# A hybrid decoder layer on one core: block substitution to 32, its scratch copies on the weights' queue, a diagonal by column sums, and steps in another order

## The chip, the cores and the metric

The kernel runs on one core of one Trainium2 chip. The metric is the device time of one launch in microseconds (us). The kernel before took 1806.01 us (median of three runs, 1805.75 to 1806.58).

## The reference, cut to what matters

One decoder layer for 256 positions of width 2048, all in fp32. Three branches (a gated DeltaNet A, an HGRN2 recurrence B, attention C into 256 memory rows) share one input projection; their outputs are projected back, gated, merged and projected again, and an MLP of width 8192 follows.

```
proj = h @ w_in[l]                        # 2048 x 15376
...
lower = where(strict, bc[..., :, None] * einsum('bhnid,bhnjd->bhnij', kc, kc) * dec, 0.0)
a_mat = lower + eye(CHUNK)
sol = lax.linalg.triangular_solve(a_mat, rhs, left_side=True, lower=True, unit_diagonal=True)   # branch A
...
a_i = einsum('bhtd,bhjd,bhtjd->bhtj', q_i, k_i, dec)                                            # branch B
o = (q_i * exp(b_i)) @ state + a_i @ v_i
...
merged = ga * (oa @ w_br_a[l]) + gb * (ob @ w_br_b[l]) + gc * (oc @ w_br_c[l])
x = x + rmsnorm(merged @ w_out[l], g_post_mix[l])
m = square(relu(h2 @ w_mlp_in[l])) @ w_mlp_out[l]
x = x + rmsnorm(m, g_post_mlp[l])
```

The change touches two pieces: the inverse of the unit triangular `a_mat` in branch A (the kernel works with chunks of 128, so one 128x128 matrix for each of 8 heads and 2 chunks), and, in branch B, the diagonal of `a_i`, where the decay is 1, so that it is the sum over d of q times k.

## The kernel before, in words

**The products with the weights.** Nearly all of the time TensorE multiplies activations with weights. Each fp32 number is split into a high and a low part (fp32r), and three products (high x high, high x low, low x high) are summed. Weights come in groups of 512 KB (two K-tiles of 128 rows by 512 columns). For each group SyncE issues one DMA into one of four raw buffers `w` (L163), ScalarE writes the high part `wh` (L174), VectorE subtracts to get the low part `wl` (L175), and both parts have four buffers of their own. A `unit` (L206 to L208) spends 12 matmuls of 128x512 on a group; a `unit_joined` (L225, L227) spends 8 of 128x512 and 8 of 128x256. All weights go through SyncE's one queue, in program order.

**The branches' own work.** Everything else of the branches (convolutions, norms, chunk matrices, recurrences) is written as Python generators. After each weight group `tick` adds a rate (R1 to R4, by stage) to a credit and runs that many steps of the generator at hand, so that small work is dealt out between the groups. A scheduler then orders each engine's instructions for itself, except those that are wrapped in `pin`. What an engine has in its list, it does in that order: a VectorE step that waits holds back the `wl` behind it.

**Branch A** (`gen_a`) runs in two halves (hg 0 and 1), each of 4 heads x 2 chunks = 8 matrices. It writes the signed strict triangles `U`, then inverts: (1) the eight 16x16 diagonal blocks `U[k,:,k]` go to a DRAM scratch `scr` (8 DMAs, L849) and come back as `Lb`, each block copied to 16 partitions (8 DMAs of 128 KB, L851), both on GpSimd's queue; (2) VectorE substitutes: 15 pairs of a product (L885) and a sum (L886), each for all heads and blocks at once; (3) TensorE transposes the result (L896), and three turns s = 16, 32, 64 double the block: `pw` (L916, for s = 64 L905), `pzt` (L921, L910), then for s < 64 eight transposes into `X` (L929), with a copy on VectorE or ScalarE behind each.

**Branch B** (`gen_b`) works in two halves too. Its diagonal comes from eight fp32 matmuls of 128x128, k against q (`ad`, L1064), of which a mask keeps the diagonal.

**The opening** makes five small turns on TensorE (`rb` by two, the gate column, `pc`, `pl`), each with a bank of its own, between the first weight groups; `dec` (L798) is a pair of matmuls with the triangle `mgtr` for each chunk.

Of the kernel before, what the change touches and what calls it, by code (L numbers as in the profile page):

```python
# [10 lines left out]
F32 = mybir.dt.float32  # L11
# [22 lines left out]
KG = 2  # L34
BL = 16
WB = 4
R1, R2, R3, R4 = 1.1, 1.0, 1.0, 1.2


@with_exitstack  # L40
def tile_trunk(ctx: ExitStack, tc, a):
# [361 lines left out]


    mgt, mlt, caus = const("mgt", [P, P]), const("mlt", [P, P]), const("caus", [P, P])
    mgtr = const("mgtr", [P, P], F32R)
    msk2 = const("msk2", [P, 2, P])
    dblk = const("dblk", [P, BL])
    mblk = const("mblk", [P, P])
    mT = {s: const(f"mT{s}", [P, P]) for s in (1, 2, 4, 8, 16, 32, 64)}  # L410

    def gen_masks():
        G.affine_select(out=mgt, in_=ones, pattern=[[-1, P]], base=0, channel_multiplier=1,
                        compare_op=ALU.is_gt, fill=0.0)
        G.affine_select(out=mlt, in_=ones, pattern=[[1, P]], base=0, channel_multiplier=-1,
                        compare_op=ALU.is_gt, fill=0.0)
        pin(V.tensor_tensor(out=caus, in0=mlt, in1=ident, op=ALU.add))
        pin(V.tensor_copy(mgtr, mgt))
        pin(V.tensor_copy(msk2[:, 0, :], mlt))
        pin(V.tensor_scalar(out=msk2[:, 1, :], in0=caus, scalar1=-1.0, scalar2=None, op0=ALU.mult))  # L420
        pin(V.tensor_reduce(out=dblk, in_=ident.rearrange("p (k c) -> p c k", c=BL), axis=AX.X, op=ALU.add))
        yield
        prev = ident
        for s in (1, 2, 4, 8, 16, 32, 64):
            b = 2 * s
            if b < P:
                cur = mblk if b == BL else cst.tile([P, P], F32, tag=f"blk{b.bit_length() % 2}", name=f"blk{b}")
# [10 lines left out]
            pin(V.tensor_tensor(out=mT[s], in0=d, in1=mlt, op=ALU.mult))  # L438
            prev = cur
            yield  # L440

# [27 lines left out]
    def gen_start():  # L469
# [14 lines left out]
        adma(lrow, a["lb_raw"][0].rearrange("(c p) -> c p", p=P))  # L484
        load_x()
        yield
        pb = bank("rb")
        for t in range(NT):
            rr = g4("rr", (P, P))
            V.tensor_scalar(out=rr, in0=ones, scalar1=rsm[:, t:t + 1], scalar2=None, op0=ALU.mult)  # L490
            T.matmul(pb[:, t * P:(t + 1) * P], rr, ident, start=True, stop=True)
        V.tensor_copy(rbm, pb[:, 0:S])
        yield
        load_x()
        turn_grow(grow, 32, 16)
        yield
        pc = bank("pc")
        T.transpose(pc[:, 0:96], crow, ident[0:96, 0:96])
        V.tensor_copy(ccol, pc[:, 0:96])
# [6 lines left out]
        pl = bank("pl")  # L506
        T.transpose(pl[:, 0:8], lrow, ident[0:8, 0:8])
# [262 lines left out]
    def gen_a(hg, kc, qc, vc, z):  # L770
# [20 lines left out]
        dec = g4("dec", (P, 8, P))  # L791
        for t in range(NT):
            dl = g4("dl", (P, 2, 4, P), F32R)
            pd = bank("dec")
            for i, l_ in enumerate((ldh, ldl)):
                V.tensor_tensor(out=dl[:, i], in0=bc(caus, 4),
                                in1=l_.bitcast(F32)[:, t, hs].unsqueeze(2).to_broadcast([P, 4, P]), op=ALU.mult)
                T.matmul(pd, mgtr, dl[:, i].rearrange("p h i -> p (h i)"), start=i == 0, stop=i == 1)  # L798
            A.activation(dec[:, t * 4:t * 4 + 4, :], pd.rearrange("p (h i) -> p h i", h=4), AF.Exp)
            yield  # L800
# [20 lines left out]
        for t in range(NT):  # L821
# [13 lines left out]
            for h in range(4):  # L835
# [5 lines left out]
                if h % 2 == 1:  # L841
                    yield

        NB = P // BL
        scr = dp.tile([NB, 8, BL, BL], F32, tag="scr", name=nm("scr"))
        Lb = lp.tile([P, 8, BL * BL], F32, tag="lb", name=nm("lb"))
        for k in range(NB):
            sl = slice(k * BL, (k + 1) * BL)
            pin(G.dma_start(scr[k].rearrange("b c m -> c b m"), U[sl, :, sl]))  # L849
        for k in range(NB):  # L850
            G.dma_start(Lb[k * BL:(k + 1) * BL].rearrange("p b m -> p (b m)"),  # L851
                        scr[k:k + 1].rearrange("k b c m -> k (b c m)").to_broadcast([BL, 8 * BL * BL]))
        yield
        ct0, cp0 = small("ct0", 4), small("cp0", 4)
        V.tensor_tensor(out=ct0, in0=cneg[:, 0:4], in1=t0e[:, hs], op=ALU.mult)
# [19 lines left out]

        X, XT, W = g4("X", (P, 8, P)), g4("XT", (P, 8, P)), g4("W", (P, 8, P))
        V.memset(W, 0.0)
        V.memset(Lb[:, :, 0:BL * BL:BL + 1], 1.0)
        Xc = lp.tile([P, 8, BL], F32, tag="xc", name=nm("xc"))
        V.tensor_copy(Xc, dblk.unsqueeze(1).to_broadcast([P, 8, BL]))  # L880
        yield
        for c in range(BL - 2, -1, -1):
            n = BL - c
            tm = lp.tile([P, 8, BL], F32, tag="tm", name=nm("tm"), bufs=2)
            V.tensor_tensor(out=tm[:, :, 0:n], in0=Xc[:, :, c:BL], in1=Lb[:, :, c * BL + c:(c + 1) * BL], op=ALU.mult)  # L885
            V.tensor_reduce(out=Xc[:, :, c], in_=tm[:, :, 0:n], axis=AX.X, op=ALU.add)  # L886
            if c % 2 == 0:
                yield
# [151 lines left out]
    def gen_b(hg, k, g, q, v, z):  # L1040
# [382 lines left out]
```

## Time and profile before

| What | Value |
|---|---|
| median of three runs | 1806.01 us (1805.75 to 1806.58) |
| the profiled execution | 1806.44 us |
| its span in the trace | 1804.7 us |
| TensorE busy | 1793.5 us, 99% of the span |
| VectorE busy | 1127.0 us, 62% |
| ScalarE busy | 905.6 us, 50% |
| mean granted clock of TensorE | 0.999 |

The profiled execution is 0.43 us above the median, and 1.7 us longer than its span. In the trace's rows, a start and a duration in us stand first, then the engine, the line, the operation and its tiles; "wl<-w,wh" reads: writes `wl`, reads `w` and `wh`. A matmul's printed duration holds its latency, and matmuls overlap; what one costs in a row of many is the distance from its start to the next one's. TensorE's fp32 matmuls are recorded twice (x16 for eight). A window's row has, for each engine, its busy us and the number of its instructions, then the granted clock, the DMA engines' busy share and the bytes moved per second.

### The profile page before, as it was taken

Reading aid. Unit: us, or ns where it says so; the run is one execution under the profiler, and the core shown is the slowest. Engines: PE = TensorE matmul, PEld = TensorE weight load, DVE = VectorE, ACT = ScalarE, POOL = GpSimd, SP = SyncE. Lnnn points to the kernel's source line nnn. Section 1 sums busy time; section 2 is a strip of 40 time slices with the busy share of each in tenths; the row PEclk is TensorE's granted clock in tenths of the full one; section 3 lists DMA queues with packets and bytes.
Section 4 is the critical chain, followed back from the end, with each engine's and each line's share of the span. In section 5 each row is a group of like instructions: output and inputs, shape, how many; then the busy total and the mean of one; then the engine's idle time right before and its main releaser. Section 6 shows DMA issues by size and latency. Waiting matters only on the chain.

```text
span 1804.7 us, 23851 instructions
## 1 busy us (share of the span) xinstructions
PE 1793.5 (99%) x9241; PEld 1532.6 (85%) x9241; DVE 1127.0 (62%) x1518; ACT 905.6 (50%) x1156; POOL 44.5 (2%) x68
## 2 busy tenths in 40 slices
PE   9999999999999999999999999999999999999998
PEld 7888888888888888888888888888888888888886
DVE  5865678755764677696555557655655565655556
ACT  6645565544555565555444445544444444444433
POOL 1000000200200000000000000000000000000000
PEclk9999999999999999999999999999999999999999
DMA  8665645754665556465666674666666676666664
GB/s 264 207 194 160 185 146 168 209 172 138 177 187 152 158 169 187 141 186 175 198 186 187 213 232 152 191 193 191 195 186 198 188 220 187 195 187 195 188 194 139
DMA packets 174946, 333.40 MB, mean 185 GB/s; under 512 B 13144, under 2 KB 14832, under 8 KB 174576
## 3 DMA queue, kind: packets, MB, share of 16 engines
q1 hardware_dynamic: 169280, 325.10, 58.7%
q10 hardware_dynamic: 4528, 4.54, 0.9%
q0 software_dynamic: 1024, 2.23, 0.7%
q8 instruction: 72, 1.18, 0.3%
q14 instruction: 42, 0.34, 0.1%
HBM read 329.60 MB, written 2.23 MB: 184 GB/s over the span
## 4 chain that ended last, share of the span: by engine, by line
PE 97%; DVE 1%; DMA 1%; ACT 1%; issue 0%; SPq 0%; DVEq 0%; POOLq 0%; POOL 0%; ACTq 0%
PE mm L225 23%; PE mm L206 18%; PE mm L207 18%; PE mm L208 18%; PE mm L227 12%; PE pa L1120 1%; DMA w<-in_w_kv_mem 0%; PE pzt L921 0%; PE pw L916 0%; PE mm L373 0%; PE mm L375 0%; PE mm L372 0%; DVE wl L175 0%; DMA w<-in_w_in 0%; DVE cv L718 0%
## 5 line engine op out<-in xcount | busy, mean ns | idle before, releaser
L175 DVE TENSOR_TENSOR wl<-w,wh 128x1024 fp32r<-128x1024 f32 x600 | 728.5, 1223 | 540.2 <-ACT wh L174 456.3
L174 ACT CAST wh<-w 128x1024 fp32r<-128x1024 f32 x600 | 628.0, 1052 | 719.0 <-PE mm L208 453.7
L206 PE MATMUL mm<-wh,hh 128*128 128x512 f32 x576 | 227.5, 395 | 0.3 <-DVE sum L266 0.3
L208 PE MATMUL mm<-wh,hh 128*128 128x512 f32 x576 | 224.7, 390 | 0.0
L225 PE MATMUL mm<-h2h,wh 128*128 128x512 f32 x960 | 224.4, 390 | 0.0
L207 PE MATMUL mm<-wl,hh 128*128 128x512 f32 x576 | 224.4, 390 | 0.0
L225 PEld LDWEIGHTS mm<-h2h,wh 128*128 128x128 f32 x960 | 178.3, 188 | 35.8
L206 PE MATMUL mm<-wh,mh 128*128 128x512 f32 x512 | 199.2, 389 | 0.0
L207 PE MATMUL mm<-wl,mh 128*128 128x512 f32 x512 | 199.2, 389 | 0.0
L208 PE MATMUL mm<-wh,ml 128*128 128x512 f32 x512 | 199.2, 389 | 0.0
L225 PE MATMUL mm<-hh,wh 128*128 128x512 f32 x768 | 184.8, 391 | 0.3 <-ACT z L730 0.3
L225 PEld LDWEIGHTS mm<-hh,wh 128*128 128x128 f32 x768 | 141.0, 188 | 27.8 <-ACT z L730 0.5
L208 PEld LDWEIGHTS mm<-wh,hh 128*128 128x128 f32 x576 | 108.1, 188 | 22.7
L206 PEld LDWEIGHTS mm<-wh,hh 128*128 128x128 f32 x576 | 108.2, 188 | 21.8 <-DVE sum L266 0.5
L207 PEld LDWEIGHTS mm<-wl,hh 128*128 128x128 f32 x576 | 108.3, 188 | 21.1
L227 PEld LDWEIGHTS mm<-h2h,wl 128*128 128x128 f32 x960 | 119.3, 192 | 2.3
L227 PE MATMUL mm<-h2h,wl 128*128 128x256 f32 x960 | 120.3, 283 | 0.0
L207 PEld LDWEIGHTS mm<-wl,mh 128*128 128x128 f32 x512 | 96.1, 188 | 20.0
L208 PEld LDWEIGHTS mm<-wh,ml 128*128 128x128 f32 x512 | 96.1, 188 | 19.9
L206 PEld LDWEIGHTS mm<-wh,mh 128*128 128x128 f32 x512 | 96.1, 188 | 19.9
L227 PE MATMUL mm<-hh,wl 128*128 128x256 f32 x768 | 102.2, 284 | 0.0
L227 PEld LDWEIGHTS mm<-hh,wl 128*128 128x128 f32 x768 | 98.9, 191 | 3.4
(388 smaller groups left out, 1913.9 us busy)
## 6 DMA issues: line engine op xcount, KB each, us to landing
w<-in_w_in SPq DMA_DIRECT2D x240, 512.0 KB, 4.0
w<-in_w_mlp_in SPq DMA_DIRECT2D x128, 512.0 KB, 4.0
w<-in_w_mlp_out SPq DMA_DIRECT2D x128, 512.0 KB, 4.2
w<-in_w_out SPq DMA_DIRECT2D x32, 512.0 KB, 4.1
w<-in_w_kv_mem SPq DMA_DIRECT2D x30, 512.0 KB, 4.9
w<-in_w_br_c SPq DMA_DIRECT2D x16, 512.0 KB, 4.1
w<-in_w_br_a SPq DMA_DIRECT2D x16, 512.0 KB, 4.5
w<-in_w_br_b SPq DMA_DIRECT2D x16, 512.0 KB, 3.6
```

What stands on the lines that cost most here:

```text
L174: q(A.copy(wh[:, js, 0:width], w[:, js, 0:width]))
L175: q(V.tensor_tensor(out=wl[:, js, 0:width], in0=w[:, js, 0:width], in1=wh.bitcast(F32)[:, js, 0:width], op=ALU.subtract))
L206: T.matmul(o, st, wh[:, j, :], start=kt == 0, stop=False)
L207: T.matmul(o, st, wl[:, j, :], start=False, stop=False)
L208: T.matmul(o, sl, wh[:, j, :], start=False, stop=kt == nk - 1)
L225: T.matmul(ps[c], wh[:, j, c * P:(c + 1) * P], both[j], start=k0 + j == 0, stop=end)
L227: T.matmul(ps[c][:, 0:S], wl[:, j, c * P:(c + 1) * P], both[j][:, 0:S], start=False, stop=end)
L1120: T.matmul(pas[h][:, t * 192:t * 192 + 192], kp[:, h, t * P:(t + 1) * P], qp[:, h * 2 + t, 0:192], start=True, stop=True)
```

## The change

- **Substitution to 32.** `substitute(1)` does what the 15 pairs did before, for all eight blocks of 16. Then the odd blocks' triangles are read again into the odd rows of `Lb`, the off-diagonal 16x16 squares of each block of 32 (in `Lx`, two tiles for 4 matrices each) are multiplied and summed, and `substitute(0)` runs 15 more pairs with that as a start. The turn s = 16 is gone: TensorE starts at s = 32 with blocks of 32.
- **Scratch on SyncE's queue.** The 8 writes to `scr` and the 8 reads of `lb` move from GpSimd to SyncE, no longer pinned. New there, for each half: 4 writes of the off-diagonal squares, 8 reads into `Lx` (32 partitions x 4 KB) and 4 re-reads of `lb` (16 partitions x 8 KB).
- **Smaller last turn.** After s = 32 only the upper left 64x64 of each `XT` is turned back: eight transposes of 64x64 in place of eight of 128x128, and one copy for two.
- **Diagonal by sums.** VectorE multiplies k by q (128x1024), splits it with ScalarE, and four fp32r matmuls of 128x512 with a matrix of ones sum over the partitions; the mask is unchanged.
- **Opening.** The five turns share one bank `cols`, one step after another group. `dec` makes both factors first, and its two matmuls stand a step later. Three masks more.
- **Rates.** R2, R3, R4 go from 1.0, 1.0, 1.2 to 1.2, 1.2, 1.27.

```diff
-R1, R2, R3, R4 = 1.1, 1.0, 1.0, 1.2
+R1, R2, R3, R4 = 1.1, 1.2, 1.2, 1.27
...
+        pt = bank("cols")
+        pg, pc, pl = pt[:, 256:288], pt[:, 288:384], pt[:, 384:392]
+        for t in range(NT):
+            T.matmul(pt[:, t * P:(t + 1) * P], rrs[t], ident, start=True, stop=True)
+        T.transpose(pg, grow, ident[0:32, 0:32])
...
+            yield
+            pd = bank("dec")
+            for i in range(2):
                 T.matmul(pd, mgtr, dl[:, i].rearrange("p h i -> p (h i)"), start=i == 0, stop=i == 1)
...
+        def spread(rows, src):
+            nc.sync.dma_start(rows, src.rearrange("k b c m -> k (b c m)").to_broadcast([rows.shape[0], rows.shape[1]]))
+
         for k in range(NB):
-            sl = slice(k * BL, (k + 1) * BL)
-            pin(G.dma_start(scr[k].rearrange("b c m -> c b m"), U[sl, :, sl]))
+            sl, w = slice(k * BL, (k + 1) * BL), k % 2 * 2
+            nc.sync.dma_start(scr[k // 2, w].rearrange("b c m -> c b m"), U[sl, :, sl])
         for k in range(NB):
-            G.dma_start(Lb[k * BL:(k + 1) * BL].rearrange("p b m -> p (b m)"),
-                        scr[k:k + 1].rearrange("k b c m -> k (b c m)").to_broadcast([BL, 8 * BL * BL]))
+            spread(Lb[k * BL:(k + 1) * BL].rearrange("p b m -> p (b m)"), scr[k // 2, k % 2 * 2:k % 2 * 2 + 1])
+        yield
+        for k in range(NB // 2):
+            r0 = 2 * k * BL
+            nc.sync.dma_start(scr[k, 1].rearrange("b c m -> c b m"), U[r0:r0 + BL, :, r0 + BL:r0 + 2 * BL])
+        for k in range(NB // 2):
+            r0 = 2 * k * BL
+            for t in range(NT):
+                spread(Lx[t][r0:r0 + 2 * BL].rearrange("p b m -> p (b m)"), scr[k, 1:2, t * 4:t * 4 + 4])
...
+        yield from substitute(1)
+
+        for k in range(NB // 2):
+            spread(Lb[(2 * k + 1) * BL:(2 * k + 2) * BL].rearrange("p b m -> p (b m)"), scr[k, 0:1])
+        V.tensor_scalar(out=Xc[:, :, 0, :], in0=Xc[:, :, 1, :], scalar1=rsecond, scalar2=None, op0=ALU.mult)
+        for t in range(NT):
+            ts = slice(t * 4, t * 4 + 4)
+            lx = Lx[t].rearrange("p b (c m) -> p b c m", c=BL)
+            V.tensor_tensor(out=lx, in0=Xc[:, ts, 0, :].unsqueeze(2).to_broadcast([P, 4, BL, BL]), in1=lx, op=ALU.mult)
+            yield
+            V.tensor_reduce(out=Xc[:, ts, 0, :], in_=lx, axis=AX.X, op=ALU.add)
+            yield
+        yield from substitute(0)
...
-        for s in (s_ for s_ in (2, 4, 8, 16, 32, 64) if s_ >= BL):
+        for s in (s_ for s_ in (2, 4, 8, 16, 32, 64) if s_ >= 2 * BL):
...
+            if s == 32:
+
+                pt = bank("X")
+                for b in range(8):
+                    T.transpose(pt[0:64, b * 64:(b + 1) * 64], XT[0:64, b, 0:64], ident[0:64, 0:64])
+                A.copy(X[0:64, :, 0:64], pt[0:64, :].rearrange("p (b i) -> p b i", b=8))
+                yield
+                continue
...
-            for h in range(4):
-                T.matmul(pd[:, h * P:(h + 1) * P], k[:, h, t * P:(t + 1) * P], q[:, h, t * P:(t + 1) * P],
-                         start=True, stop=True)
...
+        V.tensor_tensor(out=kq, in0=k.rearrange("p h s -> p (h s)"), in1=q.rearrange("p h s -> p (h s)"), op=ALU.mult)
+        yield
+        A.copy(kqh, kq)
+        V.tensor_tensor(out=kql, in0=kq, in1=kqh.bitcast(F32), op=ALU.subtract)
+        yield
+        for hp in range(2):
+            pd, cs = bank("ad"), slice(hp * 512, hp * 512 + 512)
+            T.matmul(pd, onesr, kqh[:, cs], start=True, stop=False)
+            T.matmul(pd, onesr, kql[:, cs], start=False, stop=True)
```

**SyncE, half 0.** SyncE's list before, where the last unit of branch A's projections (the gate z) is fetched; `w` are weight groups.

```order
L163 DMA w_3349<-in_w_in 128x2x512
L163 DMA w_3372<-in_w_in 128x2x512
L163 DMA w_3402<-in_w_in 128x2x512
L163 DMA w_3431<-in_w_in 128x2x512
L163 DMA w_3468<-in_w_in 128x2x512
```

The same place now, with `scr` the scratch, `lb` and `Lx` its reads:

```order
L163 DMA w_3394<-in_w_in 128x2x512
L868 DMA scr_3374<-U_3130 16x8x16 x8
L864 DMA lb_3375<-scr_3374 16x2048 x8
L874 DMA scr_3374<-U_3130 16x8x16 x4
L163 DMA w_3424<-in_w_in 128x2x512
L864 DMA Lx_3376<-scr_3374 32x1024
L864 DMA Lx_3377<-scr_3374 32x1024
...
L864 DMA Lx_3377<-scr_3374 32x1024
L163 DMA w_3446<-in_w_in 128x2x512
```

Twenty copies stand between the unit's groups 5 and 6 (`w_3394`, `w_3424`), and eight between 6 and 7 (`w_3446`).

**VectorE, half 1.** VectorE's list before, in the branch's second half, at the start of the substitution (`lb`, `tm`, `xc`), with the weights' `wl` around it:

```order
L175 TENSOR_TENSOR wl_4886<-w_4883,wh_4885 128x1024
L175 TENSOR_TENSOR wl_4936<-w_4933,wh_4935 128x1024
L175 TENSOR_TENSOR wl_4942<-w_4939,wh_4941 128x1024
L878 MEMSET lb_4584 128x8x16
L885 TENSOR_TENSOR tm_4765<-xc_4745,lb_4584 128x8x2
...
L885 TENSOR_TENSOR tm_4847<-xc_4745,lb_4584 128x8x8
L886 TENSOR_REDUCE xc_4745<-tm_4847 128x8
L175 TENSOR_TENSOR wl_4987<-w_4984,wh_4986 128x1024
```

The same place now:

```order
L175 TENSOR_TENSOR wl_4914<-w_4911,wh_4913 128x1024
L910 MEMSET lb_4719 128x8x16
L914 TENSOR_TENSOR tm_4926<-xc_4899,lb_4719 128x8x2
...
L916 TENSOR_REDUCE xc_4899<-tm_5188 128x8
L924 TENSOR_SCALAR xc_4899<-xc_4899,rsecond 128x8x16
L928 TENSOR_TENSOR Lx_4720<-xc_4899,Lx_4720 128x1024
L928 TENSOR_TENSOR Lx_4721<-xc_4899,Lx_4721 128x1024
L175 TENSOR_TENSOR wl_4962<-w_4959,wh_4961 128x1024
L175 TENSOR_TENSOR wl_4968<-w_4965,wh_4967 128x1024
```

Before, seven pairs stood between two `wl`; now all 15 pairs, L924 and the two products with `Lx` do.

**TensorE, half 0.** TensorE's list before, from the transposes of the substituted blocks on (between two of these rows stand the 12 matmuls of a weight group):

```order
L896 MATMUL XT_3768<-ident,X_3486 128x128 x4
...
L916 MATMUL pw_3795<-X_3486,U_2959 128x64 x8
...
L921 MATMUL pzt_3823<-XT_3487,W_3488 128x64 x8
...
L929 MATMUL X_3851<-ident,XT_3487 128x128 x4
L929 MATMUL X_3857<-ident,XT_3487 128x128 x4
...
L916 MATMUL pw_3881<-X_3486,U_2959 128x64 x8
```

And now:

```order
L944 MATMUL XT_4048<-ident,X_3564 128x128 x4
L964 MATMUL pw_4054<-X_3564,U_3130 128x64 x8
...
L969 MATMUL pzt_4082<-XT_3565,W_3566 128x64 x8
...
L978 MATMUL X_4113<-ident,XT_3565 64x64 x8
...
L953 MATMUL pw_4141<-X_3564,U_3130 64x64 x8
```

One `pw`, one `pzt` and eight transposes are gone, and the eight transposes that stay are 64x64.

## Rows read from the trace of the kernel before

**Rows 1.** The page: busy time by engine, and the chain that ended last

```profile
PE 1793.5 (99%) x9241; PEld 1532.6 (85%) x9241; DVE 1127.0 (62%) x1518; ACT 905.6 (50%) x1156; POOL 44.5 (2%) x68
...
PE 97%; DVE 1%; DMA 1%; ACT 1%; issue 0%; SPq 0%; DVEq 0%; POOLq 0%; POOL 0%; ACTq 0%
```

**Rows 2.** What TensorE waited for, whole span: us, times, longest

```profile
PE idle L336 <- POOL ident L84: 1.6, 1, 1.6
PE mm L373 <- DVE memT L277: 0.4, 1, 0.4
PE mm L225 <- ACT z L730: 0.3, 1, 0.3
PE mm L206 <- DVE sum L266: 0.3, 1, 0.3
```

**Rows 3.** TensorE's timeline at the turn s = 16, half 0

```profile
388.98 1.89 PE L916 MATMUL pw<-X,U 128*128 128x64 f32 x16
390.68 0.48 PE L206 MATMUL mm<-wh,hh 128*128 128x512 f32 x1
391.00 0.39 PE L207 MATMUL mm<-wl,hh 128*128 128x512 f32 x1
391.23 0.40 PE L208 MATMUL mm<-wh,hh 128*128 128x512 f32 x1
...
398.06 1.04 PE L929 MATMUL X<-ident,XT 128*128 128x128 f32 x8
...
399.16 0.39 PE L207 MATMUL mm<-wl,hh 128*128 128x512 f32 x1
```

**Rows 4.** Groups by line, TensorE: count, busy us, mean ns

```profile
L921 PE MATMUL pzt<-XT,W 128*128 128x64 f32 x64 | 7.6, 271 | 0.0
...
L929 PE MATMUL X<-ident,XT 128*128 128x128 f32 x32 | 4.1, 273 | 0.0
```

**Rows 5.** TensorE's timeline at a turn of 64x64, the diagonal, and dec

```profile
414.51 1.14 PE L905 MATMUL pw<-X,U 64*64 64x64 f32 x16
415.58 0.50 PE L206 MATMUL mm<-wh,hh 128*128 128x512 f32 x1
...
633.18 1.95 PE L1064 MATMUL ad<-sum,ft 128*128 128x128 f32 x16
634.89 1.20 PE L227 MATMUL mm<-hh,wl 128*128 128x256 f32 x8
...
275.90 0.47 PE L798 MATMUL dec<-dl,mgtr 128*128 128x512 f32 x1
276.20 0.40 PE L225 MATMUL mm<-hh,wh 128*128 128x512 f32 x1
```

**Rows 6.** Windows of the span: without copies, and while lb is read

```profile
326.00:328.00 2.00, 2.00 (x12) 1.70 (x11) 1.71 (x7) 1.68 (x3) 2.00 (x2) 1.00 0.93 327
334.00:336.00 2.00, 2.00 (x10) 1.65 (x9) 2.00 (x6) 1.06 (x1) 1.04 (x3) 1.00 1.03 131
336.00:338.00 2.00, 2.00 (x11) 1.65 (x10) 2.00 (x3) 1.01 (x2) 0.77 (x2) 1.00 0.97 120
```

**Rows 7.** Tile lb: its reads from the scratch

```profile
L851 POOL DMA_DIRECT2D lb<-scr x16: 487/487/515, 331.9 to 494.1; - x16
```

**Rows 8.** Timeline: TensorE at the start of z's unit, VectorE during it

```profile
328.56 0.40 PE L206 MATMUL mm<-wh,hh 128*128 128x512 f32 x1
...
332.84 1.22 DVE L175 TENSOR_TENSOR wl<-w,wh 128x1024 fp32r<-128x1024 f32 x1
```

**Rows 9.** Line L885 alone: duration min, median and max in ns

```profile
L885 DVE TENSOR_TENSOR tm<-xc,lb x30: 177/233/293, 358.2 to 529.1; 128x16 f32<-128x16 f32 x2, 128x24 f32<-128x24 f32 x2, 128x32 f32<-128x32 f32 x2, 128x40 f32<-128x40 f32 x2
```

**Rows 10.** Groups by line: the opening's transposes before the first products

```profile
L336 PE MATMUL idle<-ident 128*128 128x128 f32 x19 | 4.5, 424 | 1.6 <-POOL ident L84 1.6
```

**Rows 11.** Windows at the end of the span

```profile
1795.00:1800.00 5.00, 1.23 (x6) 0.69 (x4) 3.96 (x8) 0.72 (x2) 0.55 (x1) 0.98 0.55 203
1800.00:1805.00 5.00, 0.00 (x0) 0.00 (x0) 1.36 (x3) 0.00 (x0) 0.00 (x0) 0.50 0.56 210
```

More of the change, by code (lines that the diff above doesn't have):

```diff
@@ L405, in tile_trunk @@
     mgt, mlt, caus = const("mgt", [P, P]), const("mlt", [P, P]), const("caus", [P, P])
-    mgtr = const("mgtr", [P, P], F32R)
+    mgtr, onesr = const("mgtr", [P, P], F32R), const("onesr", [P, P], F32R)
     msk2 = const("msk2", [P, 2, P])
@@ L409, in tile_trunk @@
     mblk = const("mblk", [P, P])
+    rfirst, rsecond = const("rfirst", [P, 1]), const("rsecond", [P, 1])
     mT = {s: const(f"mT{s}", [P, P]) for s in (1, 2, 4, 8, 16, 32, 64)}
@@ L418, in gen_masks @@
         pin(V.tensor_copy(mgtr, mgt))
+        pin(V.tensor_copy(onesr, ones))
         pin(V.tensor_copy(msk2[:, 0, :], mlt))
@@ L426, in gen_masks @@
             if b < P:
-                cur = mblk if b == BL else cst.tile([P, P], F32, tag=f"blk{b.bit_length() % 2}", name=f"blk{b}")
+                cur = cst.tile([P, P], F32, tag=f"blk{b.bit_length() % 2}", name=f"blk{b}")
                 v3 = cur.rearrange("p (n s) -> p n s", s=b)
@@ L438, in gen_masks @@
             pin(V.tensor_tensor(out=mT[s], in0=d, in1=mlt, op=ALU.mult))
+            if s == BL:
+                pin(V.tensor_tensor(out=mblk, in0=cur, in1=mT[s], op=ALU.subtract))
+                pin(V.tensor_reduce(out=rfirst, in_=mT[s], axis=AX.X, op=ALU.add))
+                pin(V.tensor_scalar(out=rfirst, in0=rfirst, scalar1=1.0 / BL, scalar2=None, op0=ALU.mult))
+                pin(V.tensor_scalar(out=rsecond, in0=rfirst, scalar1=-1.0, scalar2=1.0, op0=ALU.mult, op1=ALU.add))
             prev = cur
@@ L486, in gen_start @@
         yield
[L487 to L492, printed above, removed]
-        yield
[L494 to L499, printed above, removed]
+        load_x()
+        yield
         for nm_, t in (("gn_a", gna), ("gn_b", gnb)):
@@ L505, in gen_start @@
         load_x()
-        pl = bank("pl")
-        T.transpose(pl[:, 0:8], lrow, ident[0:8, 0:8])
+        rrs = []
+        for t in range(NT):
+            rrs.append(g4("rr", (P, P)))
+            V.tensor_scalar(out=rrs[t], in0=ones, scalar1=rsm[:, t:t + 1], scalar2=None, op0=ALU.mult)
+        yield
[4 more added lines that the diff above has]
+        T.transpose(pg, grow, ident[0:32, 0:32])
+        T.transpose(pc, crow, ident[0:96, 0:96])
+        T.transpose(pl, lrow, ident[0:8, 0:8])
+        V.tensor_copy(rbm, pt[:, 0:S])
+        V.tensor_copy(gcol[:, 16:48], pg)
+        V.tensor_copy(ccol, pc)
         raw, e, lb = small("raw", 8), small("e", 8), small("lb", 8)
@@ L793, in gen_a @@
             dl = g4("dl", (P, 2, 4, P), F32R)
-            pd = bank("dec")
             for i, l_ in enumerate((ldh, ldl)):
@@ L844, in gen_a @@
         NB = P // BL
-        scr = dp.tile([NB, 8, BL, BL], F32, tag="scr", name=nm("scr"))
+        scr = dp.tile([NB // 2, 3, 8, BL, BL], F32, tag="scr", name=nm("scr"))
         Lb = lp.tile([P, 8, BL * BL], F32, tag="lb", name=nm("lb"))
+        Lx = [g4("Lx", (P, 4, BL * BL)) for t in range(NT)]
+        def spread(rows, src):
+            nc.sync.dma_start(rows, src.rearrange("k b c m -> k (b c m)").to_broadcast([rows.shape[0], rows.shape[1]]))
         for k in range(NB):
-            sl = slice(k * BL, (k + 1) * BL)
-            pin(G.dma_start(scr[k].rearrange("b c m -> c b m"), U[sl, :, sl]))
+            sl, w = slice(k * BL, (k + 1) * BL), k % 2 * 2
+            nc.sync.dma_start(scr[k // 2, w].rearrange("b c m -> c b m"), U[sl, :, sl])
         for k in range(NB):
-            G.dma_start(Lb[k * BL:(k + 1) * BL].rearrange("p b m -> p (b m)"),
-                        scr[k:k + 1].rearrange("k b c m -> k (b c m)").to_broadcast([BL, 8 * BL * BL]))
+            spread(Lb[k * BL:(k + 1) * BL].rearrange("p b m -> p (b m)"), scr[k // 2, k % 2 * 2:k % 2 * 2 + 1])
[7 more added lines that the diff above has]
+                spread(Lx[t][r0:r0 + 2 * BL].rearrange("p b m -> p (b m)"), scr[k, 1:2, t * 4:t * 4 + 4])
         yield
@@ L877, in gen_a @@
         V.memset(W, 0.0)
-        V.memset(Lb[:, :, 0:BL * BL:BL + 1], 1.0)
-        Xc = lp.tile([P, 8, BL], F32, tag="xc", name=nm("xc"))
-        V.tensor_copy(Xc, dblk.unsqueeze(1).to_broadcast([P, 8, BL]))
+        Xc = lp.tile([P, 8, 2, BL], F32, tag="xc", name=nm("xc"))
+        V.tensor_copy(Xc[:, :, 1, :], dblk.unsqueeze(1).to_broadcast([P, 8, BL]))
         yield
[L882 to L888, printed above, removed]
@@ L889, in gen_a, with substitute @@
-        V.tensor_tensor(out=X.rearrange("p b (k c) -> p b k c", c=BL), in0=Xc.unsqueeze(2).to_broadcast([P, 8, NB, BL]),
-                        in1=mblk.rearrange("p (k c) -> p k c", c=BL).unsqueeze(1).to_broadcast([P, 8, NB, BL]), op=ALU.mult)
+        def substitute(w):
+            pin(V.memset(Lb[:, :, 0:BL * BL:BL + 1], 1.0))
+            for c in range(BL - 2, -1, -1):
+                n = BL - c
+                tm = lp.tile([P, 8, BL], F32, tag="tm", name=nm("tm"), bufs=2)
+                V.tensor_tensor(out=tm[:, :, 0:n], in0=Xc[:, :, w, c:BL], in1=Lb[:, :, c * BL + c:(c + 1) * BL],
+                                op=ALU.mult)
+                V.tensor_reduce(out=Xc[:, :, w, c], in_=tm[:, :, 0:n], axis=AX.X, op=ALU.add)
+                if c % 2 == 0:
+                    yield
@@ new lines, in gen_a @@
+        yield from substitute(1)
+        for k in range(NB // 2):
+            spread(Lb[(2 * k + 1) * BL:(2 * k + 2) * BL].rearrange("p b m -> p (b m)"), scr[k, 0:1])
+        V.tensor_scalar(out=Xc[:, :, 0, :], in0=Xc[:, :, 1, :], scalar1=rsecond, scalar2=None, op0=ALU.mult)
+        for t in range(NT):
+            ts = slice(t * 4, t * 4 + 4)
[4 more added lines that the diff above has]
+            yield
@@ new lines, in gen_a @@
+        yield from substitute(0)
+        V.scalar_tensor_tensor(out=Xc[:, :, 0, :], in0=Xc[:, :, 1, :], scalar=rfirst, in1=Xc[:, :, 0, :],
+                               op0=ALU.mult, op1=ALU.add)
+        V.tensor_tensor(out=X.rearrange("p b (k c) -> p b k c", c=2 * BL),
+                        in0=Xc.rearrange("p b w c -> p b (w c)").unsqueeze(2).to_broadcast([P, 8, NB // 2, 2 * BL]),
+                        in1=mblk.rearrange("p (k c) -> p k c", c=2 * BL).unsqueeze(1).to_broadcast([P, 8, NB // 2, 2 * BL]),
+                        op=ALU.mult)
@@ L1060, in gen_b @@
         AT = g4("AT", (P, 8, P))
-        for t in range(NT):
-            pd = bank("ad")
-            for h in range(4):
-                T.matmul(pd[:, h * P:(h + 1) * P], k[:, h, t * P:(t + 1) * P], q[:, h, t * P:(t + 1) * P],
-                         start=True, stop=True)
-            V.tensor_tensor(out=AT.rearrange("p (h t) i -> p h t i", t=NT)[:, :, t, :],
-                            in0=pd.rearrange("p (h i) -> p h i", h=4), in1=bc(ident, 4), op=ALU.mult)
+        kq, kqh, kql = g4("kq"), g4("kqdh", dt=F32R), g4("kqdl", dt=F32R)
+        V.tensor_tensor(out=kq, in0=k.rearrange("p h s -> p (h s)"), in1=q.rearrange("p h s -> p (h s)"), op=ALU.mult)
+        yield
+        A.copy(kqh, kq)
+        V.tensor_tensor(out=kql, in0=kq, in1=kqh.bitcast(F32), op=ALU.subtract)
+        yield
+        for hp in range(2):
+            pd, cs = bank("ad"), slice(hp * 512, hp * 512 + 512)
+            T.matmul(pd, onesr, kqh[:, cs], start=True, stop=False)
+            T.matmul(pd, onesr, kql[:, cs], start=False, stop=True)
+            V.tensor_tensor(out=AT[:, hp * 4:hp * 4 + 4, :], in0=pd.rearrange("p (b i) -> p b i", b=4), in1=bc(ident, 4),
+                            op=ALU.mult)
         yield
```

## The prediction

> **What bounds the kernel now.** I read the page's busy line and chain first [rows 1]: TensorE is busy 99% of the span, and 97% of the chain that ended last is its own work. Then its waits [rows 2]: four in all, 2.6 us together, none of them on a weight. So nothing that VectorE, ScalarE or a queue does shows in the time today; the time is the sum of TensorE's instructions, and a change pays by what it takes off that list, until it makes a weight late. The third reading is the timeline around the turns that go [rows 3]. A printed duration overstates a matmul; what counts is how far the products behind are pushed. Product follows product at 0.23 us there (391.00 to 391.23).
>
> A measurement of this kernel can't tell less than some 0.2% from no change, 3.6 us; so "faster" means under 1802.4.
>
> **The change part by part: TensorE.**
>
> *The turn s = 16.* `pw` starts at 388.98, and the second product behind it at 391.00, where without it that would start 0.23 after 388.98: 391.00 - 388.98 - 0.23 = 1.79 us. `pzt` has the same shape, count and busy time (7.6 us for 64 records [rows 4]), so 1.79 too. The eight transposes: 399.16 - 398.06 - 0.23 = 0.87 [rows 3]. Together 4.45 us for a half, 8.9 for two. All of it is on the path, since TensorE waits for nothing around it.
>
> *The smaller transposes of s = 32.* The eight of 128x128 cost 0.87. The trace has sixteen records at 64x64: 415.58 - 414.51 = 1.07 us, 0.067 each [rows 5]. Eight are 0.54, and up to 0.2 for the two changes of shape: 0.54 to 0.74. I take 0.2 saved in a half, 0.4 in two.
>
> *The diagonal.* Eight fp32 matmuls push the next product by 634.89 - 633.18 = 1.71. Four of 128x512 in fp32r come in: `dec`, alike in shape and type, costs 276.20 - 275.90 = 0.30 where it stands alone [rows 5], and 0.23 in a row of products; 0.92 to 1.20 for four. Saved 0.5 to 0.8 in a half; I take 0.7, or 1.4 for two. VectorE's and ScalarE's new parts of 128x1024 lie beside TensorE.
>
> *The opening's joined turns* do the same multiplications. I allow 0.2 (0 to 0.3) for edges between shapes, two of 0.09 (390.68 to 391.00 is 0.32, against 0.23 [rows 3]).
>
> Sum: 8.9 + 0.4 + 1.4 + 0.2 = 10.9 us; with all low ends 10.2, and with the turn by busy time (half of 7.6 for each of `pw` and `pzt`) about 12. The profiled execution took 1806.44, so without any new wait 1795.5, which is 0.43 less, 1795.1, on the scale of the median.
>
> **The change part by part: what may make a weight late.** Two places.
>
> *Place 1, SyncE, half 0.* Today, while `lb` is read, the DMA engines are full and move 131 and 120 GB/s; without those reads they moved 327 at a share of 0.93 [rows 6]. So 128 KB take 1.05 us of all engines as a read of `lb` (16 partitions), and 0.40 as weights (128 partitions). The eight reads, 8.4 us, started at 331.9 [rows 7] from GpSimd, a queue of their own, and cost TensorE nothing: the `wl` of z's group 3 was done at 334.06, and the unit, started at 328.56 [rows 8] with 12 products of 0.23 a group, came to it at 328.56 + 3 x 2.73 + 0.23 = 336.98, a lead of 2.9 (the subtracted part is read by the second product). Now the copies stand in the weights' own queue: group 6 is issued behind the reads of `lb`, group 7 behind the eight of `Lx`. With the reads where they were: engines free at 331.9 + 8.4 = 340.3; group 6 (four times 0.40) 341.9; eight `Lx`; group 7 another 1.6; splitting 2.4 on ScalarE and VectorE (the subtraction 1.22 [rows 8], the cast taken alike). An `Lx` read has 128 KB, 32 partitions, 4 KB in each. Its bounds are 0.40 and 1.05. If what slows `lb` is how many bytes go into one partition, it is half of 1.05; the nearest row is `lb`'s, read by that, and I take 0.52. Then group 7 is split at 340.3 + 1.6 + 4.2 + 1.6 + 2.4 = 350.1. TensorE wants it at 328.56 + 7 x 2.73 + 0.23 = 347.9, and later by the 12 small products of 128x256 that the list puts among these groups, 0.13 each (8 in 1.03 us behind 634.89 fits that), 1.5: at 349.4. Late by 0.7 us. With `Lx` at 0.40 it is in time; with 1.05 late by 4.9.
>
> [...]
>
> *Place 2, VectorE, half 1.* All 15 pairs, L924 and both `Lx` products now stand between two `wl`. A product takes 177 to 293 ns, median 233 [rows 9], the sums alike: 30 x 0.233 = 7.0, less by overlap, say 6.3; two products of 128x1024 at 1.22: 2.4. So the `wl` behind comes some 8.7 us later, and four more with one sum over 128x1024, taken at 1.22 as well, among them follow in 6.1: the last at 14.8. TensorE has from the last `wl` before the block its lead L, and then four groups of 8 x 0.23 + 8 x 0.13 = 2.8, some 11.2. Late by 3.6 - L. With a lead as at z, 2.9, that is 0.7; but the load in front of this block now stands behind the reads of `lb`, so I take half the lead, 1.4: late by 2.2. Ends: 0 (a lead over 3.6) and 8 (the load itself late by the time of the copies).
>
> *Half 0's VectorE and half 1's queue* have the same instructions in other company, and the four later re-reads of `lb`, 4.2 us of engines, come when weights take 1.6 us of the engines in every 2.7; I count them at nothing, hidden by the groups' leads, with the same lead gone as their price (it is in the 8 above).
>
> [...]
>
> The other new work (second substitution, 6 to 7 us in a half; products and sums with `Lx`, 4.9) falls on VectorE, busy 62%: covered unless it comes in one block. The `dec` step, masks and rates move work by a group or so; nothing waits there now.
>
> Sum: 1806.44 - 10.9 + 0.7 + 2.2 = 1798.4 in the profiled execution; on the median 1798.0.
>
> **The rivals.**
>
> *No wait at all*: 1795.1. For it: not one wait on a weight in the whole span, even while DMA ran at 120 GB/s. Against: the lead there is 2.9, and each block is 8 us or more.
>
> *The waits eat the gain.* `Lx` at `lb`'s 1.05 (4.9 at place 1) and place 2 with no lead (3.6): 1795.1 + 8.5 = 1803.6; with place 2 at 8, 1808.0. For it: the only row of such a copy is the slow one. Against: half the bytes for a partition.
>
> [...]
>
> *The change does not do what it says*, that is, TensorE's freed time is filled at once because weights, not products, set the pace: then about 1806. Against: no wait on weights, and a group takes 1.6 us of the engines where one is wanted every 2.7. It counts with the second rival.
>
> **How the numbers follow.** No wait 0.27; the forecast, 1796.5 to 1802.4, 0.38; gain eaten, 1802.4 to 1809.6, 0.21; slower 0.14. So faster 0.65, same 0.21, slower 0.14. The range leaves out little below (all of the high sum of savings, 1794) and the far part of the waits above: 1794.3 to 1808.5; the forecast's own range is 1796.5 to 1802.4.
>
> **What would show it.** In the changed trace: TensorE's records down by some 100 and its busy time by 10 to 11 us; no row for the s = 16 turn; the diagonal's four products at 0.23 to 0.30. TensorE's waits would have a row on `wl` (or ScalarE's `wh`) of 1 to 5 us in place 1's unit, and one in half 1's. SyncE's `Lx` reads: windows of 128 KB in 0.5 us. I am wrong if waits on weights stay under 0.5 us, if they pass 8 us, if the granted clock has a dip inside the branches, or if TensorE's list shrinks by other than 10 to 12 us.

## The result, and the profile after

The changed kernel takes 1813.76 us (median of five, 1813.10 to 1815.69), the kernel before 1806.58 beside it: a ratio of 1.0043 (95% interval 1.0031 to 1.0054). It is slower by some 7 us. The forecast was 1798.0 with a range to 1808.5. The profiled execution, from which the rows below come, took 1815.69 us, the slowest of the five.

The page of the kernel after, the two rows that answer to [rows 1]:

```profile
PE 1789.9 (99%) x9137; PEld 1522.6 (84%) x9137; DVE 1152.7 (64%) x1599; ACT 904.0 (50%) x1150; POOL 24.7 (1%) x36
...
PE 93%; DVE 2%; DMA 2%; ACT 1%; issue 1%; POOL 0%; SPq 0%; ACTq 0%; DVEq 0%; POOLq 0%
```

TensorE has 104 records fewer, but the chain now runs through VectorE and DMAs for 4% of the span where that was 2%. What TensorE waited for (us, times, longest), to be read against the four rows of [rows 2]:

```profile
PE mm L227 <- DVE wl L175: 4.2, 4, 2.4
PE mm L206 <- ACT wh L174: 3.9, 2, 2.8
PE mm L207 <- DVE wl L175: 1.8, 4, 0.8
...
PE mm L206 <- DVE sum L266: 1.5, 1, 1.5
PE mm L225 <- ACT wh L174: 0.9, 1, 0.9
```

2.6 us of waits have become 15.4, and most are on weights, which before were never waited for. To find where, I took the 8128 products with weights, which are the same in number and order in both traces, and subtracted start from start. The profiled execution falls 3.7 us behind in the opening (product 1 to 61), 7.5 between the first product of z's unit and its end (place 1), and ends 9.3 behind (last product at 1805.13 against 1795.84). Within a stretch I also summed how far each start-to-start distance exceeds the median of its form: opening 4.0 us, place 1 (340 to 366) 7.6, place 2 (515 to 545) 7.0, and 1.7 for one wait at 568; before, the first three stretches had 0.2, 0.0 and 0.1.

**Place 1.** SyncE's timeline at z's unit in the kernel after (start, length of the run of issues), then what SyncE waited for between 320 and 365:

```profile
319.72 7.00 SPq L163 DMA_DIRECT2D w<-in_w_in  x4
332.38 5.24 SPq L868 DMA_DIRECT2D scr<-U  x8
337.66 3.66 SPq L864 DMA_DIRECT2D lb<-scr  x8
341.37 2.74 SPq L874 DMA_DIRECT2D scr<-U  x4
344.89 0.39 SPq L163 DMA_DIRECT2D w<-in_w_in  x1
347.90 3.56 SPq L864 DMA_DIRECT2D Lx<-scr  x8
351.57 11.25 SPq L163 DMA_DIRECT2D w<-in_w_in  x8
```

```profile
SPq L868 <- DVE AQ L850: 5.9, 1, 5.9
...
SPq L864 <- DMA scr<-U: 2.5, 1, 2.5
```

No weight is issued from 326.7 to 344.9. Until 337.4 that is not the queue's doing. All four raw buffers are taken, and the one for z's group 6 comes free with this subtraction of VectorE's:

```profile
336.23 1.22 DVE L175 TENSOR_TENSOR wl<-w,wh 128x1024 fp32r<-128x1024 f32 x1
```

So the 5.9 us that SyncE waits for VectorE to finish U hold back no weight by themselves. From 337.4 on, group 6 stands behind the eight reads of `lb` (first at 337.66) and the four small writes, 7.4 us. Group 7 stands, besides, behind 2.5 us in which SyncE waits for those small writes to land before `Lx` is read, and behind the eight issues of `Lx`; it is issued at 351.57. Windows of the same stretch (engines' busy us and counts, granted clock, DMA share, GB/s):

```profile
332.00:334.00 2.00, 2.00 (x11) 1.63 (x10) 1.35 (x5) 1.24 (x3) 1.49 (x1) 1.00 0.08 8
...
342.00:344.00 2.00, 2.00 (x11) 1.65 (x10) 1.47 (x4) 1.06 (x1) 0.00 (x0) 1.00 1.05 131
...
350.00:352.00 2.00, 1.24 (x8) 0.84 (x6) 1.23 (x1) 2.00 (x8) 0.00 (x0) 1.00 1.03 238
```

At 332 the DMA engines are 8% busy, since no buffer is free for a weight and `lb` cannot be read yet. At 342 they are full with the reads of `lb` alone, at 131 GB/s as before [rows 6]; at 350 with those of `Lx` alone, at 238. ScalarE's cast of group 7, TensorE's timeline at that last group of z, and the clock there:

```profile
356.01 1.04 ACT L174 CAST wh<-w 128x1024 fp32r<-128x1024 f32 x1 [4.00 <-DMA w<-in_w_in]
```

```profile
353.91 0.39 PE L208 MATMUL mm<-wh,hh 128*128 128x512 f32 x1
357.11 0.79 PE L206 MATMUL mm<-wh,hh 128*128 128x512 f32 x1 [2.81 <-ACT wh L174]
358.37 0.79 PE L207 MATMUL mm<-wl,hh 128*128 128x512 f32 x1 [0.47 <-DVE wl L175]
358.96 0.63 PE L208 MATMUL mm<-wh,hh 128*128 128x512 f32 x1
359.38 0.63 PE L206 MATMUL mm<-wh,hh 128*128 128x512 f32 x1
```

```profile
355.00:360.00 5.00, 2.43 (x5) 1.63 (x6) 2.58 (x3) 3.15 (x3) 0.00 (x0) 0.66 1.04 347
360.00:365.00 5.00, 5.00 (x17) 3.92 (x16) 3.71 (x4) 2.59 (x5) 0.00 (x0) 0.66 0.92 302
```

After the wait the products stand 0.43 us apart, not 0.23, and the granted clock is 0.50 from 357 to 363. That makes up some 2.5 of the 7.6 us.

**Place 2.** The timeline of TensorE, VectorE, SyncE and ScalarE in half 1 of the kernel after, a few rows of each; VectorE's 30 operations of the substitution fill the time from 522.93 to 530.94:

```profile
522.73 1.21 PE L227 MATMUL mm<-hh,wl 128*128 128x256 f32 x8 [0.34 <-DVE wl L175]
522.74 0.17 DVE L910 MEMSET lb<- 128x128 f32 x1
...
523.04 13.25 SPq L163 DMA_DIRECT2D w<-in_w_in  x6
...
527.42 1.04 ACT L174 CAST wh<-w 128x1024 fp32r<-128x1024 f32 x1 [6.01 <-DMA w<-in_w_in]
...
528.52 3.92 PE L225 MATMUL mm<-hh,wh 128*128 128x512 f32 x16 [0.93 <-ACT wh L174]
...
531.26 2.36 DVE L928 TENSOR_TENSOR Lx<-xc,Lx 128x1024 f32<-128x1024 f32 x2
...
533.54 2.35 DVE L175 TENSOR_TENSOR wl<-w,wh 128x1024 fp32r<-128x1024 f32 x2
...
534.81 2.35 PE L227 MATMUL mm<-hh,wl 128*128 128x256 f32 x16 [2.37 <-DVE wl L175]
```

The block lasts from 522.74 to 533.54, 10.8 us. ScalarE's part of the next weight was ready from 528.5; VectorE's subtraction starts five us later. The queue has a part here too: TensorE waits 0.3 us for the `wl` in front of the block, and 0.9 for the `wh` behind it, whose weight is issued at 523.04, behind this half's copies, though its buffer was free from 507.8. Here the granted clock stays at 1.00, in each window of 5 us from 520 to 545.

**The opening.** ScalarE's timeline of the kernel after, and then of before (its own DMA issues carry "ACTq"):

```profile
38.92 0.44 ACTq L94 DMA_DIRECT2D dtb<-in_dt_bias  x1
39.46 2.94 ACT L174 CAST wh<-w 128x1024 fp32r<-128x1024 f32 x3 [3.51 <-DMA x<-in_x]
```

```profile
35.97 1.04 ACT L174 CAST wh<-w 128x1024 fp32r<-128x1024 f32 x1
38.44 0.35 ACTq L94 DMA_DIRECT2D gnb<-in_gn_b  x1
```

Before, the cast ran ahead of three of the four small loads, of which the first waits for a load of x; now it stands behind all four. TensorE waits 0.5 and 1.1 us, and the granted clock falls afterwards, to 0.76 over 40 to 45, with 0.50 from 43 on:

```profile
40.00:45.00 5.00, 4.45 (x16) 3.57 (x17) 4.47 (x9) 3.73 (x6) 0.00 (x0) 0.76 0.70 234
```

### The profile page after: what moved, and what is told of

Read it like the earlier page. It is cut to its first block, busy times and chain, and to the rows that moved or that the text cites. A ratio compares the mean times of both kernels' runs of the same rounds, so it can differ in the third digit from the quotient of the medians.

```text
span 1813.9 us, 23731 instructions
## 1 busy us (share of the span) xinstructions
PE 1789.9 (99%) x9137; PEld 1522.6 (84%) x9137; DVE 1152.7 (64%) x1599; ACT 904.0 (50%) x1150; POOL 24.7 (1%) x36
## 4 chain that ended last, share of the span: by engine, by line
PE 93%; DVE 2%; DMA 2%; ACT 1%; issue 1%; POOL 0%; SPq 0%; ACTq 0%; DVEq 0%; POOLq 0%
PE mm L225 23%; PE mm L206 18%; PE mm L207 18%; PE mm L208 18%; PE mm L227 12%; DMA w<-in_w_kv_mem 1%; PE pa L1181 1%; DVE wl L175 1%; DMA w<-in_w_in 1%; DMA x<-in_x 0%; ACT wh L174 0%; PE tr L1319 0%; DVE tm L914 0%; PE ab L677 0%; DVE xc L916 0%
```

## The experiments

Each ran beside the kernel before, whose median was 1806.1 to 1806.2 us.

**The opening alone undone.**

```diff
-        pt = bank("cols")
-        pg, pc, pl = pt[:, 256:288], pt[:, 288:384], pt[:, 384:392]
...
+        pb = bank("rb")
...
+        turn_grow(grow, 32, 16)
...
+        pc = bank("pc")
+        T.transpose(pc[:, 0:96], crow, ident[0:96, 0:96])
+        V.tensor_copy(ccol, pc[:, 0:96])
         for nm_, t in (("gn_a", gna), ("gn_b", gnb)):
```

> The changed kernel with the opening of before (four turns, each with its bank, the four small ScalarE loads a step later). Theory: in the changed opening ScalarE's cast stands behind the four small loads, one of which waits for a load of x; TensorE waits 1.5 us there and then runs about 3 us at half clock, 3.7 us against before. Undone: 1810 us, and no window under 0.95 of granted clock between 35 and 50 us. Rival (the dip comes from the other parts, such as the new masks on VectorE): 1813 to 1814.

1812.11 us (six runs), 1.65 less than the changed kernel. In its trace no granted clock is under 0.95 between 35 and 50 us, and that stretch loses 0.2 us, not 4.0. The loss goes with the opening, but the profiled execution had overstated it: with the same opening, the run with pinned products (below) waited 0.4 and 0.3 us, kept its clock at 1.00 from 35 to 50, and lost 1.6 us there. It seems to depend on when x lands: the small load had waited for it until 38.04 in the changed kernel, and until 36.49 there.

**The copies on GpSimd's queue.**

```diff
-            nc.sync.dma_start(rows, src.rearrange("k b c m -> k (b c m)").to_broadcast([rows.shape[0], rows.shape[1]]))
+            G.dma_start(rows, src.rearrange("k b c m -> k (b c m)").to_broadcast([rows.shape[0], rows.shape[1]]))
...
-            nc.sync.dma_start(scr[k // 2, w].rearrange("b c m -> c b m"), U[sl, :, sl])
+            pin(G.dma_start(scr[k // 2, w].rearrange("b c m -> c b m"), U[sl, :, sl]))
...
-            nc.sync.dma_start(scr[k, 1].rearrange("b c m -> c b m"), U[r0:r0 + BL, :, r0 + BL:r0 + 2 * BL])
+            G.dma_start(scr[k, 1].rearrange("b c m -> c b m"), U[r0:r0 + BL, :, r0 + BL:r0 + 2 * BL])
```

> The changed kernel with all of branch A's scratch copies, the new ones too, on GpSimd's queue. Theory (head of line): weights are late at 351 to 364 because SyncE stands behind copies that wait for U and for one another, while the DMA engines are idle; on another queue the 4.6 us of waits and 3.0 us of half clock there go: 1801 to 1806 us, the waits near 523 to 540 us (VectorE's block of pairs) partly left. Rival (bytes): the copies take the engines from the weights on any queue; waits stay, 1811 to 1814.

1807.9 us (1805.2 to 1814.1, ten runs; the profiled execution 1811.19). No wait and no dip is left at z's unit, and one of 1.9 us on a `wl` stands in the unit behind it. SyncE's issue of group 6, GpSimd's reads of `lb`, and ScalarE's cast of group 7:

```profile
337.84 0.37 SPq L163 DMA_DIRECT2D w<-in_w_in  x1
...
338.16 3.86 POOL L864 DMA_DIRECT2D lb<-scr  x8
...
348.74 1.05 ACT L174 CAST wh<-w 128x1024 fp32r<-128x1024 f32 x1 [4.17 <-DMA w<-in_w_in]
```

`lb` is read no sooner than on SyncE's queue, but group 6 is issued as soon as its buffer is free, and group 7's cast starts 7.3 us sooner (348.74 against 356.01). So what made the weights late is their place behind the copies in one queue, not, by themselves, the bytes or the time at which U is done; the rival falls. The idle DMA engines of the theory are there mostly before 337.4, when no weight could have been fetched. The time is above what I expected; a new wait stands in half 1, TensorE's timeline:

```profile
521.98 3.78 PE L225 MATMUL mm<-hh,wh 128*128 128x512 f32 x8 [5.54 <-DVE mg L1064]
```

VectorE waits there to clear the diagonal of `lb` until the copies have landed, and the gate product `mg` is behind it.

**Both.**

> Both: scratch copies on GpSimd's queue and the opening of before. Theory: the two add, 1797.5 to 1802.5 us, with what VectorE's block still costs. Rival (bytes): 1807 to 1810.

1805.85 us (ten runs): the two add, but the wait on `mg` (5.1 us) and its dip in the clock, some 2 us at half clock, stay, so neither number was met.

**The rates of before.**

```diff
-R1, R2, R3, R4 = 1.1, 1.2, 1.2, 1.27
+R1, R2, R3, R4 = 1.1, 1.0, 1.0, 1.2
```

> The changed kernel with rates R2, R3, R4 of before (1.0, 1.0, 1.2). In VectorE's list of half 1 at most 11 of the 30 operations of a substitution then stand between two subtractions, where there are 30 and more. Theory (block): the 5.1 us of waits at 523 to 540 us shrink to under 1.5, the waits of half 0 stay: 1809 to 1811 us. Rival (queue there too, weights late behind Lx): they stay, 1813 to 1815.

1816.41 us (four runs), a miss. Half 1's waits do shrink, to 1.2 us, as the block theory says. But branch B then isn't through in time, TensorE's timeline:

```profile
863.62 5.33 PE L1181 MATMUL pa<-qp,kp 128*128 128x192 f32 x16 [7.06 <-DVE qp L1172]
```

The change has more steps than before; as I read it, the higher rates pay for them, and pack VectorE's work closer.

**The products of the substitution pinned.**

```diff
-                V.tensor_tensor(out=tm[:, :, 0:n], in0=Xc[:, :, w, c:BL], in1=Lb[:, :, c * BL + c:(c + 1) * BL],
-                                op=ALU.mult)
+                pin(V.tensor_tensor(out=tm[:, :, 0:n], in0=Xc[:, :, w, c:BL], in1=Lb[:, :, c * BL + c:(c + 1) * BL],
+                                    op=ALU.mult))
```

> The changed kernel with each product of the substitution pinned behind what is written before it on VectorE, so that in half 1 at most seven operations stand between two subtractions of weights, not 33. Rates and queues as changed. Theory (VectorE's block is the cause of the waits at 522 to 540 us): these shrink from 5.1 to under 1.5 us, the rest stays: 1809 to 1811 us. Rival (the weights come late behind the copies): the waits stay at 4 us and more, 1812.5 to 1815.

1807.65 us (ten runs), 6.1 less than the changed kernel and below the range expected; in its profile the opening, which the edit does not touch, loses 2.4 us less. The stretch from 500 to 545 loses 2.7 us (the changed kernel 7.0 from 515 on), and the wait at 568 is down from 1.5 to 0.2. Z's unit still loses 7.1. The block was the cause of most of the loss at place 2; of the waits that stay, 0.8 us are on a `wh` whose weight was issued late, behind the copies.

**GpSimd's queue, old opening, pinned products.**

> Copies on GpSimd's queue, the opening of before, and the pinned products. With copies on GpSimd and the old opening the trace has one wait of 5.1 us on mg (VectorE, behind a block of pairs) and some 2 us of half clock behind it, and one of 1.6 us on a wl. Theory: all three go, since nothing but blocks on VectorE was left: 1796 to 1799.5 us. Rival (TensorE's list has not shrunk by what was reckoned, waits only hid it): 1802 and more.

1802.32 us (ten runs), ratio 0.9979 (0.9970 to 0.9988): faster than before, not as far as expected. One wait is left, VectorE's and TensorE's timeline:

```profile
511.94 0.17 DVE L908 MEMSET lb<- 128x128 f32 x1 [6.54 <-DMA scr<-U]
...
514.59 1.65 PE L225 MATMUL mm<-hh,wh 128*128 128x512 f32 x3 [3.66 <-DVE mg L1062]
```

It loses 5.5 us with its dip (a granted clock of 0.73 from 515 to 520). Its last product starts at 1791.28, 4.6 before that of the kernel before, so without that loss it would be 10 ahead.

**Two small parts alone, on the kernel before** (diagonal by sums, 64x64 transposes).

> The kernel before with two parts alone: the diagonal by sums, and 64x64 transposes after s = 32. By the prediction's terms 1.4 and 0.4 us less: 1804 to 1804.6 against 1806.2. Rival: a new wait on VectorE or ScalarE for k times q, or an order moved elsewhere, takes it back: 1806 and more.

1805.90 us (ten runs), ratio 0.9998 (0.9989 to 1.0008). Start against start, the transposes give 0.11 us in each half and the diagonal 1.38 in two, where the terms were 0.4 for both halves and 1.4. Then most is given back at the branch's end, so the rival is the nearer; as I read it, the rates of before do not pay for the diagonal's two more steps:

```profile
868.15 0.30 PE L766 MATMUL oT<-ident,on 128*128 128x128 f32 x1 [1.77 <-DVE on L757]
```

**The copies on SyncE's queue alone, on the kernel before.**

```diff
-            pin(G.dma_start(scr[k].rearrange("b c m -> c b m"), U[sl, :, sl]))
+            nc.sync.dma_start(scr[k].rearrange("b c m -> c b m"), U[sl, :, sl])
...
-            G.dma_start(Lb[k * BL:(k + 1) * BL].rearrange("p b m -> p (b m)"),
+            nc.sync.dma_start(Lb[k * BL:(k + 1) * BL].rearrange("p b m -> p (b m)"),
```

> The kernel before with its 16 scratch copies a half on SyncE's queue, nothing else. Theory (head of line): SyncE issues no weight for 10 us and more while it waits for U and the copies; without the reads into Lx the delay is some 4 us shorter than in the changed kernel, whose TensorE waited 4.6 us here: 0 to 3 us of waits, 1806 to 1810. Rival (bytes): as many bytes as before, so no wait, 1806.2 within 0.4.

1814.01 us (four runs), ratio 1.0043 (1.0026 to 1.0060): this part alone costs as much as the whole change, with no byte more than before. Neither expectation holds, since the loss comes by a way that neither names. SyncE's, ScalarE's and TensorE's timelines:

```profile
330.19 4.58 SPq L851 DMA_DIRECT2D lb<-scr  x8
334.87 24.79 SPq L163 DMA_DIRECT2D w<-in_w_in  x9
...
342.95 0.37 ACT L864 ACTIVATE off<-kk,ct 128x128 f32<-128x128 f32 x1 [4.78 <-PE kk L606]
...
346.41 0.37 ACT L864 ACTIVATE off<-kk,ct 128x128 f32<-128x128 f32 x1 [2.32 <-PE kk L606]
...
349.43 3.96 ACT L174 CAST wh<-w 128x1024 fp32r<-128x1024 f32 x4
...
350.61 0.80 PE L206 MATMUL mm<-wh,hh 128*128 128x512 f32 x1 [3.36 <-ACT wh L174]
```

Here the weights had landed (no DMA moved a byte from 346 to 352), and ScalarE never waited for one: their place behind the copies made none of them late. What cost the time is ScalarE's list, which had been built anew, presumably because the scheduler reckons the weights late: four casts stand behind `off` and `nv`, which need TensorE's `kk` and `vT`; before, casts stood between them (`off`, cast at 347.22, `off`). In the changed kernel this second way counts for little. Group 6's cast runs there behind an `off` that waited 5.65 us for `kk`, but its weight landed only at 348.91, and the cast started at 349.16; group 7's waited 4.0 for its DMA. So the two losses (some 7 us in the stretch from 340 to 366 here, 7.6 there) have different causes, and their like size is chance.

**The substitution later**, on the version with GpSimd's queue, the old opening and the pinned products: two, three and four steps.

```diff
+        for _ in range(2):
+            yield
         yield from substitute(1)
```

> As the run with copies on GpSimd, old opening and pinned products, and the substitution begins two steps later. There VectorE waited 6.5 us with the clearing of lb's diagonal for copies that had not landed, mg stood behind it, and TensorE waited 3.7 us for mg, then ran some 3 us at half clock: 5.2 us in all. Theory: two steps, some 5 us, cover most of it: 1797 to 1800 us. Rival (the steps are missing at the branch's end, as with the old rates): 1802 to 1808.

1801.56 us (nine runs), ratio 0.9976 (0.9966 to 0.9986), the fastest, though not beyond the interval of the version without the two steps; it lies between the two expectations. The wait on `mg` is gone; what TensorE waits for in its place:

```profile
PE mm L225 <- DVE sum L266: 1.3, 1, 1.3
PE mm L206 <- DVE sum L266: 1.1, 1, 1.1
PE mm L207 <- DVE wl L175: 0.8, 1, 0.8
```

> The same with three steps. Theory: no wait on mg or a wl over 0.5 us, 1796.5 to 1799 us. Rival (steps missing at the end): 1802 to 1810.

1804.19 us (ten runs): a wait of 2.3 us on `sum` at 532, a dip in the clock with it (0.66 from 530 to 535), and 1.8 at the branch's end.

> The same with four steps. Theory: as with three if the branch's end holds, 1796.5 to 1799 us; if steps are missing there, a wait of TensorE of several us near 860 us and 1802 to 1810.

1806.30 us (ten runs): 5.7 us on `sum` at 532, and 1.8 at the end near 868. Both times lie in the rivals' range, and steps do seem to run short at the end; but the longer wait, on `sum`, had not been foreseen.

## Why the prediction was wrong

**TensorE's list: right.** The term of 10.9 us holds to within 1 us. The version with GpSimd's queue and pinned products is 4.6 us ahead in spite of one loss of 5.5 us; the sum is 10.1. TensorE's busy time fell by 3.6 us only in the changed kernel, where products at a granted clock of 0.50 have a printed duration of 0.63 us, not 0.39, and by 9.3 in that version. The diagonal measured 1.4 as reckoned; the smaller transposes 0.2, not 0.4.

**Place 1, the step that failed.** That weights come late behind the copies in SyncE's queue was the mechanism forecast, and the run with the copies on GpSimd's queue shows it. The sum that made group 7 late by 0.7 us failed in three terms:

- *The start of the reads.* I took the reads of `lb` "where they were", from 331.9, which is 3.4 us after z's unit begins. In the changed kernel they begin 6.1 us after it (at 337.66; the unit at 331.61), because VectorE finishes U 2.7 us later in the unit. The queue is not the reason: on GpSimd's they begin 6.2 us after it.
- *The way from there to group 7.* I reckoned 18.2 us until its low part is ready, for bytes and splitting alone. It took 20.6 (to 358.3), with 2.5 us in which SyncE waits for small writes to land. The prediction never named what SyncE itself would wait for. The bytes were taken well: 0.52 us for an `Lx`, where 238 GB/s make it 0.55. That the bytes in one partition set it was my supposition, and no run shows it.
- *The low clock behind the wait.* The sum has no term for it; at a granted clock of 0.50, from 357 to 363, it took some 2.5 us.

TensorE came to group 7 1.9 us later than reckoned, since group 6, reckoned in time, was itself 1.0 late and more small products stood there; group 7 was still 4.0 late. In all 7.6 us were lost, 4.0 of them waits as the rows print them.

**Place 2: right mechanism, size off.** Late by 2.2 us was forecast, 7.0 lost. The block lasted 10.8 us, where 8.7 were reckoned (the 30 operations took 8.0 us, 522.93 to 530.94, not 6.3). The lead, of which I took half, was gone, since the load stood behind the copies: the sum's 3.6 without a lead and the block's 2.1 more make 5.7 of the 7.0.

**The opening: not priced.** I allowed 0.2 us of gain for edges and didn't look at the order of ScalarE's list, in which three more DMA issues now stand ahead of a cast. It costs 1.65 us in the median.

**The rivals.** "Slower", over 1809.6, had 14% of chance, and 1813.76 was measured. "The waits eat the gain" had the direction: its far case, 4.9 at place 1 and 8 at place 2, gives 1808.0. There 7.6 and 7.0 were lost, so place 2 stayed inside its 8. But place 1's loss did not come by `Lx` at the rate of `lb` (238 GB/s against 131), some 2.5 of it came by the granted clock of 0.50, and the opening is in no rival. "No wait at all" fell with 15.4 us of waits. Two of the prediction's own signs of being wrong are there: waits on weights of some 11 us, over its 8, and a dip of the clock inside the branches, to 0.50.

## What to carry to other kernels

In the changed kernel the weights behind the copies in SyncE's queue came after them: group 6, whose buffer was free at 337.4, was issued at 344.89. When a DMA moves to a queue that feeds the bottleneck, price the whole row of copies from the time at which the next buffer is free: their bytes, their issues, and the waits between them, which here came to 2.5 us ahead of one weight. Take their start from the changed kernel's lists, not from the old trace. Where a scheduler builds the lists, one moved queue rebuilds the others too: compare the order of casts, copies and issues on every engine that feeds TensorE, the opening included. In one run here that cost some 7 us, with the weights in time. A gain of 11 us in the bottleneck's own list stands only if the engines around it still deliver in small pieces: pinning each step of a long chain between the weights' work was worth some 6 us on the changed kernel, as much as the queue, and 3.5 on the version with GpSimd's queue and the old opening.

## What the runs showed of the hardware

A wait could cost more than it lasted: in the changed kernel, after 2.8 us without products, the granted clock was 0.50 from 357 to 363, and products stood 0.43 us apart, not 0.23; a wait of 2.4 us at 534 left it at 1.00. Before, it was 0.50 at the end of the span, where no product ran [rows 11]. Whether a wait was followed by a dip also differed between two kernels with one opening: after 0.4 and 0.3 us the clock stayed at 1.00 from 35 to 50, after 0.5 and 1.1 it was 0.76 from 40 to 45. The times of such a kernel spread from 1805.2 to 1814.1 for the copies on GpSimd, against 1805.65 to 1806.88 for the kernel before; whether the dips are the cause was not tested. Reads into 32 partitions moved 1.8 times the bytes per second of those into 16: 238 against 131 GB/s, in windows of the changed kernel (350 to 352, 342 to 344) that carried nothing else of size.
